# Attention units with transposes in the middle of a slot, three transpose banks and one bank for all value sums

## The chip, the cores and the metric

The kernel runs on one core of a Trainium2 chip. The metric is device time in microseconds (us) of one execution, lower is better. Three runs of the kernel before took 2541.85 us in the median (2540.91 to 2544.57).

The engines in the views are PE (matmul; PEld is its weight load), DVE (vector), ACT (scalar), POOL and SP, which here issues most DMAs. PSUM is the memory that PE writes its results to; it has eight banks, each holding 512 float32 values in each of 128 partitions.

## What is computed

One decoder layer over 2048 tokens of width 1024: an adaLN-modulated RMSNorm, one wide projection, attention in eight heads of width 64 beside a short gated convolution, an output projection, and a convolutional feed-forward part. The change touches the attention alone:

```
fcum = jnp.cumsum(logf, axis=1)
for i in range(s // BLOCK_Q):                       # 16 blocks of 128 queries
    q0, q1 = i * BLOCK_Q, (i + 1) * BLOCK_Q
    logits = jnp.einsum('bqhd,bkhd->bhqk', q[:, q0:q1], k[:, :q1]) * scale
    logits = logits + fcum[:, :, q0:q1, None] - fcum[:, :, None, :q1]
    p = softmax(where(causal, logits, -inf))
    out[i] = jnp.einsum('bhqk,bkhd->bqhd', p, v[:, :q1])
```

Query block i sees i + 1 key blocks of 128. Precision is kept by splitting operands into a high and a low half, so that one product becomes two or three matmuls.

## The kernel before

**Units and slots.** The attention walks over 64 units: head h (eight of them) and u from 0 to 7. A unit pairs query block 15 - u with query block u, so every unit has 17 key blocks of 128. Each unit passes four stages, and the stages of different units share one slot: in slot s (the loop at the end of the attention block) the scores of unit s, the exponentials of unit s - 1, the transposes of unit s - 2 and the value sums of unit s - 4 are written out. Each stage is a Python generator, and the loop takes one step of each in turn ("round 1", "round 2" and so on), in the order in which they stand in the list `run`. The calls marked `K` keep that order on each engine; so the order of the list and the places of the `yield`s set the order of work on PE, DVE and ACT.

**Scores** (L778 to L802). For each chunk of up to 512 keys PE makes two matmuls into a bank of `ps_s` (four banks), and a third one for the causal mask on the last chunk of a query block (L781). DVE adds the forget term and keeps the running maximum (L802). There are five chunks in every unit. PE writes chunks in pairs, one or two ahead of DVE.

**Weights** (L816, L819). ACT scales the maximum (`nb`) and takes two exponentials in place, one for each query block of the pair, with their sums in `l`.

**Turn** (from L825). The weights must be transposed for the value sums. The last eight of the 17 blocks go through POOL (L830, L831 make a high and a low half in `wide`) and a transposing DMA on SP (L832). The first nine blocks go through PE: transposes of 4, 4 and 1 blocks into banks of `ps_x` (L839, inside `blocks`), an ACT copy of the high half out of the bank (L841) and a DVE subtraction for the low half (L846, inside `rest`). Below these are called T0, T4, T8; copy0, copy4, copy8; low0, low4, low8. `ps_x` has two banks, so a new transpose waits for the low half of the one two back.

**Values** (L878 to L880). Three matmuls for each of the 17 blocks add up the value sums of the pair: one bank of `ps_o` (two banks) for each query block. DVE multiplies each with 1/l and writes it to `at` (L869, the function `over`), which is called the eviction below.

**Store** (L895 to L898). After every second head the finished `at` is transposed in four chunks of 512, one in each of four slots: four transposes in a `ps_x` bank, an ACT copy to `tm` (one buffer) and a DMA to `m_at`. `ps_s`, `ps_x` and `ps_o` take eight banks together.

**Other queues.** SP carries, in order, the transposing DMAs, the loads of the next head, the stores and weight loads for the following stage; POOL carries L830 and L831, two copies for each head (L594) and products for the following stage (L675).

Of the kernel before, what the change touches and what calls it, by code (L numbers as in the profile page):

```python
# [8 lines left out]
F32 = mybir.dt.float32  # L9
F32R = mybir.dt.float32r  # L10
F16 = mybir.dt.float16
# [3 lines left out]
ALU = mybir.AluOpType  # L15
AX = mybir.AxisListType
PSUM = bass.MemoryType.PSUM
DRAM = bass.MemoryType.DRAM

P = 128  # L20
# [3 lines left out]
DH = 64  # L24
# [3 lines left out]
NT = S // P  # L28
# [5 lines left out]
WU = (NT + 1) * P  # L34
WB = 9
# [9 lines left out]
def kernel(  # L45
# [20 lines left out]
    V, A, G, T = nc.vector, nc.scalar, nc.gpsimd, nc.tensor  # L66
# [69 lines left out]
    K = tc.keep_in_program_order  # L136
# [10 lines left out]
    with ExitStack() as ph:  # L147
# [32 lines left out]
        with ExitStack() as pa:  # L180
# [110 lines left out]
            for k in range(KD + 2):  # L291
# [4 lines left out]
                if k < KD:  # L296
                    rest = transpose_in(0, k)
# [20 lines left out]
            for ch in range(4):  # L318
# [7 lines left out]
                for t in range(4):  # L326
                    i = ch * 4 + t
# [413 lines left out]
    with ExitStack() as ph:  # L741
        cs = ph.enter_context(tc.tile_pool(name="cs", bufs=6))
        cp = ph.enter_context(tc.tile_pool(name="cp", bufs=2))
        ps_s = st.enter_context(tc.tile_pool(name="ps_s", bufs=4, space=PSUM, side="right"))
        ps_x = ph.enter_context(tc.tile_pool(name="ps_x", bufs=2, space=PSUM))
        ps_o = ph.enter_context(tc.tile_pool(name="ps_o", bufs=2, space=PSUM))

        def load_values(pr):

            v16 = cp.tile([P, NT, 2, P], F16, tag="v16", name="v16")  # L750
            nc.sync.dma_start(v16, v16_sc[pr].rearrange("(t p) a d -> p t a d", p=P))
            return v16

        v16 = [load_values(0)]

        chunks = []
        heads = {0: head}
# [54 lines left out]
        def weights(un):  # L812

            s_t = un["s"]
            nb = cs.tile([P, 2], F32, tag="nb", name="nb")
            K(A.activation(nb, un["mx"], AF.Copy, scale=qk[:, 5:6], bias=LN_PS))  # L816
            for p, (_, n, b0) in enumerate(un["parts"]):
                cols = s_t[:, b0 * P : (b0 + n) * P]
                K(A.activation(cols, cols, AF.Exp, bias=nb[:, p : p + 1], scale=qk[:, 4:5], accum_out=un["l"][:, p : p + 1]))  # L819
                yield  # L820
            un["wide"] = wide = cp.tile([P, 2, WU - WB * P], F16, tag="wide", name="wide", bufs=3)

        def turn(un):

            s_t = un["s"]  # L825
            near = cp.tile([P, 2, WB, P], F16, tag="near", name="near", bufs=3)
            far = cp.tile([P, 2, NT + 1 - WB, P], F16, tag="far", name="far", bufs=3)
            un["t"] = near, far
            wide = un["wide"]
            K(G.tensor_scalar(wide[:, 0, :], s_t[:, WB * P : WU], 1.0, 0.0, op0=ALU.mult, op1=ALU.add))  # L830
            K(G.tensor_tensor(wide[:, 1, :], s_t[:, WB * P : WU], wide[:, 0, :], op=ALU.subtract))  # L831
            nc.sync.dma_start_transpose(far.rearrange("p a b n -> p (a b) n"), wide.rearrange("p a n -> p (a n)"))  # L832
            late = []

            def blocks(b0):
                nb = min(4, WB - b0)
                pt = ps_x.tile([P, 512], F32, tag="x", name="pt")
                for b in range(nb):
                    K(T.transpose(pt[:, b * P : (b + 1) * P], s_t[:, (b0 + b) * P : (b0 + b + 1) * P], ident))  # L839
                th, tl = [near[:, a, b0 : b0 + nb, :].rearrange("p b n -> p (b n)") for a in range(2)]  # L840
                K(A.activation(th, pt[:, 0 : nb * P], AF.Copy))  # L841
                late.append((tl, pt[:, 0 : nb * P], th))

            def rest():
                tl, pt, th = late.pop(0)
                K(V.tensor_tensor(tl, pt, th, op=ALU.subtract))  # L846

            blocks(0)
            blocks(4)
            yield  # L850
            rest()
            yield
            blocks(8)
            rest()
            yield
            rest()
            yield
            K(V.reciprocal(un["l"], un["l"]))

        def values(un):  # L860

            near, far = un["t"]
            h = un["h"]
            sums = []

            def over():
                p, i, po = sums.pop(0)
                o = un["at"][:, i, (h % 2) * DH : (h % 2 + 1) * DH]
                K(V.tensor_scalar(o, po, un["l"][:, p : p + 1], None, op0=ALU.mult))  # L869

            for p, (i, n, b0) in enumerate(un["parts"]):
                po = ps_o.tile([P, DH], F32, tag="o", name="po")
                for b in range(n):
                    g = b0 + b
                    t = near[:, :, g, :] if g < WB else far[:, :, g - WB, :]
                    v = v16[h // 2][:, b, h % 2, :]
                    vh, vl = v[:, 0:DH], v[:, DH:P]
                    K(T.matmul(po, lhsT=t[:, 0, :], rhs=vh, start=b == 0, stop=False))  # L878
                    K(T.matmul(po, lhsT=t[:, 0, :], rhs=vl, start=False, stop=False))
                    K(T.matmul(po, lhsT=t[:, 1, :], rhs=vh, start=False, stop=b == n - 1))  # L880
                    if b % 4 == 3:
                        yield
                        if sums:
                            over()
                sums.append((p, i, po))
            yield
            while sums:
                over()

        def store(at, pr, chs):  # L890

            for ch in chs:
                pt = ps_x.tile([P, 512], F32, tag="x", name="pt")
                for t in range(4):
                    K(T.transpose(pt[:, t * P : (t + 1) * P], at[:, ch * 4 + t, :], ident))  # L895
                tm = cp.tile([P, 512], F32, tag="tm", name="tm", bufs=1)
                K(A.activation(tm, pt, AF.Copy, scale=vi))
                nc.sync.dma_start(m_at[pr][:, ch * 512 : (ch + 1) * 512], tm)  # L898
                yield
# [4 lines left out]
        for s in range(H * nu + 8):  # L904
            h, u = divmod(s, nu)
            run = []
            if h < H:
                if u == 0:
# [3 lines left out]
                    if h % 2 == 0:  # L912
                        if h:
                            v16.append(load_values(h // 2))
                        at = cp.tile([P, NT, P], F32, tag="at", name="at")
                elif h + 1 < H:
                    steps[u - 1]()
                units.append({"h": h, "u": u, "at": at})
            for back, stage in ((2, turn), (0, scores), (1, weights), (4, values)):
                if 0 <= s - back < H * nu:  # L920
                    run.append(stage(units[s - back]))
            if s >= 16 and s % 16 in (0, 4):
                slow.append(store(units[s - 5]["at"], (s - 16) // 16, (0, 3) if s % 16 == 0 else (1, 2)))
# [331 lines left out]
```

## Time and profile before

| | us |
|---|---|
| median of three runs | 2541.85 |
| the profiled execution, its own time | 2541.82 |
| its span in the trace | 2540.1 |
| attention: from the first `nb` (628.55) to the last (973.85) | 345.30 |
| PE busy, DVE busy, ACT busy in that stretch | 307.18, 300.26, 267.44 |

A page of the profile gives busy times over the whole span; answers of the trace give the same for a window, list single instructions, and tell what ended each idle time. "L846 <- ACT near L841" means that the instruction of line 846 waited, and that the last thing it waited for was ACT's write of `near` in line 841. A matmul's row is longer than the distance to the next one, since matmuls overlap; the distance between starts is what one costs. Slots are told apart by the start of `nb` (L816), of which there is one for each unit.

### The profile page before, as it was taken

How to read it: one execution, taken by the hardware profiler on the slowest of the kernel's cores; microseconds unless marked ns; L12 is line 12 of the kernel's file. 1: busy time of each engine (PE TensorE's matmuls, PEld its weight loads, DVE VectorE, ACT ScalarE, POOL GpSimd, SP SyncE). 2: the span in 40 equal slices, each digit the busy share in tenths (PEclk: the TensorE clock that was granted, in tenths of full speed). 3: DMA queues.
4: the chain of work that ended last, by engine and by line, in shares of the span. 5: the costliest groups of instructions: out<-in, count | busy, mean ns of one | idle time of the engine just before them, and what ended most of it. 6: DMA issues, size and time to landing. Idle time of an engine off the chain costs nothing.

```text
span 2540.1 us, 38347 instructions
## 1 busy us (share of the span) xinstructions
PE 2429.5 (96%) x14429; PEld 1988.7 (78%) x14429; DVE 1827.2 (72%) x3422; ACT 1147.2 (45%) x1804; POOL 375.7 (15%) x314
## 2 busy tenths in 40 slices
PE   4999999999989888998999999999999999999999
PEld 4988788887666666877788888887778888888887
DVE  7567874432988886676888888667768888885554
ACT  3522331111778775654444444455534444444333
POOL 4110111111767773110000000000000000000000
PEclk9999999999999999999999999999999999999999
DMA  8332563313799886243222222676742222226775
GB/s 239 141 103 60 149 184 102 97 59 110 145 177 184 167 176 160 81 147 121 75 80 87 83 81 86 204 226 217 218 138 83 83 83 83 83 84 199 225 235 186
DMA packets 416674, 345.62 MB, mean 136 GB/s; under 512 B 182928, under 2 KB 326632, under 8 KB 415464
## 3 DMA queue, kind: packets, MB, share of 16 engines
q1 hardware_dynamic: 409304, 326.33, 45.9%
q10 hardware_dynamic: 4752, 8.46, 0.9%
q0 software_dynamic: 2432, 8.39, 0.9%
q8 instruction: 113, 1.85, 0.3%
q14 instruction: 73, 0.60, 0.1%
HBM read 244.47 MB, written 65.08 MB: 122 GB/s over the span
## 4 chain that ended last, share of the span: by engine, by line
PE 49%; DVE 2%; DMA 1%; ACT 1%; issue 0%; SPq 0%; DVEq 0%; ACTq 0%
PE acc L1103 33%; PE acc L140 15%; DMA t<-x_sc 1%; DVE lo L663 1%; PE pt L991 0%; DVE t L984 0%; DVE t L974 0%; ACT hi L662 0%; DVE t L973 0%; ACT junk L1014 0%; DVE lo L1058 0%; DVE raw L1052 0%; DMA out_dram<-t 0%; DVE b22l L663 0%; SPq L1199 0%
## 5 line engine op out<-in xcount | busy, mean ns | idle before, releaser
L140 PE MATMUL acc<-hi 128*128 128x512 f32 x960 | 378.7, 395 | 10.3 <-ACT hi L662 8.0
L140 PE MATMUL acc<-hi,lo 128*128 128x512 f32 x960 | 376.0, 392 | 1.7 <-DVE lo L663 1.6
L140 PE MATMUL acc<-lo,hi 128*128 128x512 f32 x960 | 375.4, 391 | 0.3 <-DVE lo L663 0.3
L663 DVE TENSOR_TENSOR lo<-raw,hi 128x1024 fp32r<-128x1024 f32 (+1 forms) x208 | 236.0, 1140 | 181.1 <-ACT hi L662 180.6
L662 ACT ACTIVATE hi<-raw 128x1024 fp32r<-128x1024 f32 (+1 forms) x208 | 205.1, 991 | 248.4 <-PE acc L140 206.1
L1116 DVE SCALAR_TENSOR_TENSOR w<-w,fcw,w 128x1024 f32<-128x1024 f32 x176 | 225.8, 1283 | 35.5 <-ACT w L1111 32.2
L1055 ACT ACTIVATE hi<-raw 128x1024 fp32r<-128x1024 f32 x132 | 139.7, 1060 | 211.5 <-PE acc L1103 202.9
L140 PEld LDWEIGHTS acc<-hi 128*128 128x128 f32 x960 | 181.0, 189 | 50.4 <-ACT hi L662 9.2
L140 PEld LDWEIGHTS acc<-hi,lo 128*128 128x128 f32 x960 | 180.8, 188 | 41.7 <-DVE lo L663 3.7
L140 PEld LDWEIGHTS acc<-lo,hi 128*128 128x128 f32 x960 | 181.0, 188 | 37.3 <-DVE lo L663 1.2
L1058 DVE TENSOR_TENSOR lo<-raw,hi 128x1024 fp32r<-128x1024 f32 x132 | 160.9, 1220 | 11.0 <-ACT hi L1055 10.9
L819 ACT ACTIVATE s_t<-s_t,nb,cst 128x2048 f32<-128x2048 f32 (+15 forms) x128 | 164.7, 1287 | 5.7
L140 PE MATMUL pr<-hh,wh 128*128 128x512 f32 x384 | 153.3, 399 | 0.0
L140 PE MATMUL pr<-hl,wh 128*128 128x512 f32 x384 | 151.0, 393 | 0.0
L140 PE MATMUL pr<-hh,wl 128*128 128x512 f32 x384 | 150.7, 392 | 0.0
L846 DVE TENSOR_TENSOR near<-pt,near 128x512 f16<-128x512 f32 (+1 forms) x192 | 106.1, 554 | 44.5 <-ACT near L841 43.2
L831 POOL TENSOR_TENSOR wide<-s_t,wide 128x1024 f16<-128x1024 f32 x64 | 136.6, 2134 | 5.3
L839 PE MATMUL pt<-ident,s_t 128*128 128x128 f32 x576 | 96.9, 288 | 35.0 <-DVE near L846 23.4
L802 DVE CUSTOM_DVE_ANT_0 s_t<-ps,nf,mx 128x512 f32<-128x512 f32 (+1 forms) x192 | 122.7, 639 | 1.2
L778 PE MATMUL ps<-kh,qs 128*128 128x512 f16 (+1 forms) x320 | 111.8, 354 | 2.2 <-ACT bt L635 1.1
L841 ACT ACTIVATE near<-pt 128x512 f16<-128x512 f32 (+1 forms) x192 | 87.2, 480 | 59.0 <-PE pt L839 57.9
L779 PE MATMUL ps<-kl,qs 128*128 128x512 f16 (+1 forms) x320 | 111.9, 354 | 0.0
(303 smaller groups left out, 6200.9 us busy)
## 6 DMA issues: line engine op xcount, KB each, us to landing
raw<-in_w_up_dram SPq DMA_DIRECT2D x88, 512.0 KB, 3.6
raw<-y_sc SPq DMA_DIRECT2D x176, 256.0 KB, 4.0
raw<-in_w_down_dram SPq DMA_DIRECT2D x176, 256.0 KB, 4.3
y_sc<-w SPq DMA_DIRECT2D x44, 512.0 KB, 2.6
wm<-in_w_ada_dram SPq DMA_DIRECT2D x128, 128.0 KB, 2.5
wr<-in_w_in_dram SPq DMA_DIRECT2D x40, 256.0 KB, 4.0
x_t<-in_x_dram SPq DMA_DIRECT2D x16, 512.0 KB, 5.1
wa<-in_w_ada_dram SPq DMA_DIRECT2D x16, 512.0 KB, 6.4
```

Of the source, the lines that this page charges most:

```text
L140: ins = T.matmul(acc, lhsT=a, rhs=b, start=st, stop=sp)
L662: A.activation(hi, raw, AF.Copy, scale=HS)
L663: V.tensor_tensor(lo, raw, hi.bitcast(F32), op=ALU.subtract)
L778: K(T.matmul(ps[:, 0:cw], lhsT=qt, rhs=kh[:, c0 : c0 + cw], start=True, stop=False))
L779: K(T.matmul(ps[:, 0:cw], lhsT=qt, rhs=kl[:, c0 : c0 + cw], start=False, stop=not last))
L802: K(V.tensor_tensor_reduce(out=s_t[:, o0 + c0 : o0 + c0 + cw], in0=ps[:, 0:cw], in1=nf[:, c0 : c0 + cw], scale=1.0, scalar=-3.0e38 if g == ...
L819: K(A.activation(cols, cols, AF.Exp, bias=nb[:, p : p + 1], scale=qk[:, 4:5], accum_out=un["l"][:, p : p + 1]))
L831: K(G.tensor_tensor(wide[:, 1, :], s_t[:, WB * P : WU], wide[:, 0, :], op=ALU.subtract))
L1055: K(A.activation(hi, raw, AF.Copy, scale=HS))
L1058: K(V.tensor_tensor(lo, raw, hi.bitcast(F32), op=ALU.subtract))
L1103: K(T.matmul(acc, lhsT=a, rhs=b, start=st, stop=sp, skip_group_check=True))
L1116: K(V.scalar_tensor_tensor(y, u[:, m : m + 1024], fcw[:, m * 44 + ct : m * 44 + ct + 1], y, op0=ALU.mult, op1=ALU.add))
```

## The change

The pools: `ps_x` gets three banks and `ps_o` one. That one bank is allocated once and cut into four pieces of 2 x 64 columns, used by the units in turn; both query blocks of a unit lie in one piece, and one DVE instruction (L885 after the change) multiplies both with their 1/l. `wide` goes from three buffers to two and `tm` from one to two. In the list, the exponentials come first and the transposes after the scores; the transposes' steps are moved to later rounds.

```diff
@@ -742,8 +742,8 @@
-        ps_x = ph.enter_context(tc.tile_pool(name="ps_x", bufs=2, space=PSUM))
-        ps_o = ph.enter_context(tc.tile_pool(name="ps_o", bufs=2, space=PSUM))
+        ps_x = ph.enter_context(tc.tile_pool(name="ps_x", bufs=3, space=PSUM))
+        ps_o = ph.enter_context(tc.tile_pool(name="ps_o", bufs=1, space=PSUM))
@@ -752,6 +752,8 @@
+        ring = ps_o.tile([P, 512], F32, name="po").rearrange("p (a b d) -> p a b d", b=2, d=DH)
+        rings = [ring[:, a] for a in range(4)]
@@ -818,7 +820,7 @@
-            un["wide"] = wide = cp.tile([P, 2, WU - WB * P], F16, tag="wide", name="wide", bufs=3)
+            un["wide"] = wide = cp.tile([P, 2, WU - WB * P], F16, tag="wide", name="wide", bufs=2)
@@ -845,31 +847,28 @@
+            yield
+            K(V.reciprocal(un["l"], un["l"]))
+            yield
             blocks(0)
+            yield
             blocks(4)
-            yield
-            rest()
             yield
             blocks(8)
             rest()
             yield
             rest()
             yield
-            K(V.reciprocal(un["l"], un["l"]))
+            rest()
 
         def values(un):
-            sums = []
-
-            def over():
-                p, i, po = sums.pop(0)
-                o = un["at"][:, i, (h % 2) * DH : (h % 2 + 1) * DH]
-                K(V.tensor_scalar(o, po, un["l"][:, p : p + 1], None, op0=ALU.mult))
-
+            rings.append(rings.pop(0))
+            po2 = rings[0]
             for p, (i, n, b0) in enumerate(un["parts"]):
-                po = ps_o.tile([P, DH], F32, tag="o", name="po")
+                po = po2[:, p, :]
                 for b in range(n):
@@ -880,12 +879,10 @@
                     if b % 4 == 3:
                         yield
-                        if sums:
-                            over()
-                sums.append((p, i, po))
-            yield
-            while sums:
-                over()
+            yield
+            u = un["u"]
+            o = un["at"][:, NT - 1 - u : u - 1 if u else None : 2 * u + 1 - NT, (h % 2) * DH : (h % 2 + 1) * DH]
+            K(V.tensor_tensor(o, po2, un["l"].unsqueeze(2).broadcast_to([P, 2, DH]), op=ALU.mult))
@@ -893,7 +890,7 @@
-                tm = cp.tile([P, 512], F32, tag="tm", name="tm", bufs=1)
+                tm = cp.tile([P, 512], F32, tag="tm", name="tm", bufs=2)
@@ -916,7 +913,7 @@
-            for back, stage in ((2, turn), (0, scores), (1, weights), (4, values)):
+            for back, stage in ((1, weights), (0, scores), (2, turn), (4, values)):
```

Three places show what moves. The first is ACT in the middle of the attention, before the change: `near<-pt` is copy0, copy4 (128x512) or copy8 (128x128), and `s_t,l<-` are the exponentials.

```order
L819 ACTIVATE s_t,l<-s_t,nb,cst 128x1280
L819 ACTIVATE s_t,l<-s_t,nb,cst 128x896
L841 ACTIVATE near<-pt 128x128
L841 ACTIVATE near<-pt 128x512 x2
L816 ACTIVATE nb<-mx,cst 128x2
L819 ACTIVATE s_t,l<-s_t,nb,cst 128x1152
L819 ACTIVATE s_t,l<-s_t,nb,cst 128x1024
```

The same place on ACT after the change:

```order
L821 ACTIVATE s_t,l<-s_t,nb,cst 128x1280
L821 ACTIVATE s_t,l<-s_t,nb,cst 128x896
L843 ACTIVATE near<-pt 128x512 x2
L843 ACTIVATE near<-pt 128x128
L818 ACTIVATE nb<-mx,cst 128x2
L821 ACTIVATE s_t,l<-s_t,nb,cst 128x1152
L821 ACTIVATE s_t,l<-s_t,nb,cst 128x1024
```

Before, the copy8 of one unit stands right ahead of copy0 and copy4 of the next one; now the three copies of one unit stand together behind the exponentials.

The second place is DVE in one slot, before the change: `s_t,mx<-ps` are the scores' chunks, `near<-pt,near` low0, low4 and low8, and `at<-po,l` the evictions.

```order
L802 ISA s_t,mx<-ps,nf 128x512
L802 ISA mx 128x1
L846 TENSOR_TENSOR near<-pt,near 128x512
L802 ISA s_t,mx<-ps,nf 128x512
L802 ISA mx 128x1
L846 TENSOR_TENSOR near<-pt,near 128x512
L802 ISA s_t,mx<-ps,nf,mx 128x512
L802 ISA mx 128x1
L846 TENSOR_TENSOR near<-pt,near 128x128
L802 ISA s_t,mx<-ps,nf,mx 128x512
L802 ISA mx 128x1
L858 RECIPROCAL l<-l 128x2
```

DVE after the change, from the fourth chunk of one slot to the first of the next:

```order
L804 ISA s_t,mx<-ps,nf,mx 128x512
L804 ISA mx 128x1
L804 ISA s_t,mx<-ps,nf,mx 128x128
L804 ISA mx 128x1
L848 TENSOR_TENSOR near<-pt,near 128x512 x2
L885 TENSOR_TENSOR at<-po,l 128x2x64
L848 TENSOR_TENSOR near<-pt,near 128x128
L804 ISA s_t,mx<-ps,nf 128x512
```

The low halves were spread between the chunks of scores; now they stand behind the last chunk, with the one eviction among them. In half of the units the eviction stands behind low4, as here, in the other half between low0 and low4.

The third place is PE at the start of a slot, before the change: the end of a unit's sums (`far`), two chunks of scores, eight transposes (T0 and T4 together), and the next unit's first sum (`near`).

```order
L880 MATMUL po<-v_7526,far 128x64
L778 LDWEIGHTS qs
L778 MATMUL ps<-kh,qs 128x512
L779 LDWEIGHTS qs
L779 MATMUL ps<-kl,qs 128x512
L778 LDWEIGHTS qs
L778 MATMUL ps<-kh,qs 128x512
L779 LDWEIGHTS qs
L779 MATMUL ps<-kl,qs 128x512
L839 MATMUL pt<-ident,s_t 128x128 x8
L878 LDWEIGHTS near
L878 MATMUL po<-v_7526,near 128x64
```

PE after the change, at the end of a slot: T8, the last block of a unit's sums and the first block of the next unit's.

```order
L841 MATMUL pt<-ident,s_t 128x128
L877 LDWEIGHTS far
L877 MATMUL po<-v_7491,far 128x64
L878 LDWEIGHTS far
L878 MATMUL po<-v_7491,far 128x64
L879 LDWEIGHTS far
L879 MATMUL po<-v_7491,far 128x64
L877 LDWEIGHTS near
L877 MATMUL po<-v_7491,near 128x64
```

The transposes have left the start of the slot for its third, fourth and fifth round. In two units of eight, those with u = 0 and u = 4, nothing stands between the last sum of one unit and the first of the next, and in the built program that first sum of each unit now waits for the eviction of the unit just before it, whose sums lie in the same bank.

## The prediction

> **What bounds the kernel now.** The page first, for the size of the question.
>
> ```profile
> span 2540.1 us, 38347 instructions
> PE 2429.5 (96%) x14429; PEld 1988.7 (78%) x14429; DVE 1827.2 (72%) x3422; ACT 1147.2 (45%) x1804; POOL 375.7 (15%) x314
> PE 49%; DVE 2%; DMA 1%; ACT 1%; issue 0%; SPq 0%; DVEq 0%; ACTq 0%
> ```
>
> PE is busy for 96% of the span and leads the chain that ended last. But this is a mean over stages, and the change touches one of them, so I cut that stage out: windows from the first to the last `nb` of the attention, over one head without stores (eight units), and over single slots.
>
> ```profile
> core 0: us, PE busy (x) PEld busy (x) DVE busy (x) ACT busy (x) POOL busy (x), PEclk, DMA share, GB/s
> 628.55:973.85 345.30, 307.18 (x4423) 231.14 (x4423) 300.26 (x998) 267.44 (x515) 244.89 (x156) 0.98 0.87 171
> 752.14:793.78 41.64, 37.77 (x577) 28.73 (x576) 38.20 (x129) 32.96 (x65) 29.22 (x19) 1.00 0.83 153
> 822.10:830.75 8.65, 5.53 (x63) 4.10 (x62) 5.19 (x17) 4.78 (x10) 8.31 (x6) 0.85 1.13 232
> 830.75:838.04 7.29, 7.29 (x87) 5.46 (x86) 4.92 (x16) 4.09 (x10) 4.18 (x4) 0.71 0.58 112
> ```
>
> The second row is the quiet head: 41.64 / 8 = 5.205 us for a unit, in which PE is busy for 4.72, DVE for 4.78, ACT for 4.12 and POOL for 3.65. No engine is full, so a chain between engines sets the pace. The first row has 63 units: at 5.205 they would take 327.9, so 17.4 us are lost in a few slots, such as the two of the last rows. Who waits for whom in the quiet head:
>
> ```profile
> ACT near L841 <- PE pt L839: 8.4, 9, 1.4
> PE pt L839 <- DVE near L846: 3.6, 7, 0.7
> DVE near L846 <- ACT near L841: 3.2, 5, 0.8
> PE po L878 <- DVE at L869: 0.3, 1, 0.3
> ```
>
> This is a ring. ACT's copies wait for PE's transposes, these for a bank that DVE's low half has to free, and the low half waits for ACT's copy. ACT's rows show the round:
>
> ```profile
> 813.47 0.69 ACT L819 ACTIVATE s_t<-s_t,nb,cst 128x384 f32<-128x384 f32 x1
> 814.16 0.25 ACT L841 ACTIVATE near<-pt 128x128 f16<-128x128 f32 x1
> 814.75 1.34 ACT L841 ACTIVATE near<-pt 128x512 f16<-128x512 f32 x2 [0.33 <-PE pt L839]
> 815.98 0.29 ACT L816 ACTIVATE nb<-mx,cst 128x2 f32<-128x2 f32 x1
> ```
>
> copy8 comes behind the exponentials; low8 follows it; with two banks T4 of the next unit needs the bank that low8 frees; copy4 needs T4; and the next exponentials stand behind copy4. So ACT's 4.12 us of work plus about 1.05 of waiting for transposes (8.4 / 8) give nearly all of the 5.205.
>
> **The change part by part.**
>
> *Three banks and the new order.* With three banks T0, T4 and T8 wait for low0, low4 and low8 of the unit before, a whole slot old, and the exponentials no longer stand between copy8 and the copies that follow from it. The ring is gone. What is late next? ACT needs 4.12, so the candidates are PE and DVE. PE, from the distances between starts:
>
> ```profile
> 809.10 0.38 PE L778 MATMUL ps<-kh,qs 128*128 128x512 f16 x1
> 809.31 0.38 PE L779 MATMUL ps<-kl,qs 128*128 128x512 f16 x1
> 809.53 0.22 PE L781 MATMUL ps<-maskb,ident_b 128*128 128x128 bf16 x1
> 809.59 1.04 PE L839 MATMUL pt<-ident,s_t 128*128 128x128 f32 x8
> 810.66 0.19 PE L878 MATMUL po<-v,near 128*128 128x64 f16 x1
> 810.97 0.19 PE L880 MATMUL po<-v,near 128*128 128x64 f16 x1
> 811.00 0.38 PE L778 MATMUL ps<-kh,qs 128*128 128x512 f16 x1
> ```
>
> A score matmul of 512 columns costs 0.215, a mask 0.06, eight transposes 1.07 (0.134 each), and the twelve sums from 810.66 to 811.00 cost 0.34 (0.0285 each). A unit has 17 x 128 = 2176 columns twice, so 2 x 4.25 x 0.215 = 1.83, two masks 0.12, nine transposes 1.21 and 51 sums 1.46: **4.62 us of PE**. Nothing in the change alters this work.
>
> *One eviction for two.* DVE has now, by its rows in time, and by the view of one line:
>
> ```profile
> 809.45 0.29 DVE L846 TENSOR_TENSOR near<-pt,near 128x128 f16<-128x128 f32 x1 [1.43 <-ACT near L841]
> 809.66 0.74 DVE L802 CUSTOM_DVE_ANT_0 s_t<-ps,nf,mx 128x512 f32<-128x512 f32 x1
> ...
> 810.32 0.28 DVE L869 TENSOR_SCALAR at<-po,l 128x64 f32<-128x64 f32 x1
> 810.52 0.15 DVE L858 RECIPROCAL l<-l 128x2 f32<-128x2 f32 x1
> ...
> 811.79 0.68 DVE L846 TENSOR_TENSOR near<-pt,near 128x512 f16<-128x512 f32 x1
> 812.39 0.68 DVE L802 CUSTOM_DVE_ANT_0 s_t<-ps,nf 128x512 f32<-128x512 f32 x1
> ```
>
> ```profile
> L517 DVE TENSOR_TENSOR qn<-acc,r x32: 683/692/694, 168.7 to 359.4; 128x512 f32<-128x512 f32 x32
> ```
>
> An eviction holds DVE for 0.20 (810.32 to 810.52), two of them 0.40. The new form, a product of a PSUM tile with a broadcast column, is not in the trace at 128 columns. At 512 it takes 692 ns (L517, which is such a product), the same as low0's 0.68 at 512 columns; low8 has 128 columns and holds DVE for 0.21 (809.45 to 809.66). The bounds are 0.20, one old eviction, and 0.69, L517 whole; I take 0.21 since size and kind match low8. DVE falls from 4.78 to 4.59 a unit, below PE's 4.62 plus waits. So the saved 0.19 is hidden by PE, and would cost up to 0.3 more if it came out at 0.69 (only then would DVE be the bound). The reciprocal only moves.
>
> *One bank for all sums: an added wait.* The first sum of each unit now waits for the eviction of the unit before, and PE runs in order, so score chunks and transposes queue behind that sum, and DVE's chunks behind them. What a bare handover costs:
>
> ```profile
> 973.53 0.47 DVE L869 TENSOR_SCALAR at<-po,l 128x64 f32<-128x64 f32 x2
> 973.86 0.19 PE L878 MATMUL po<-v,near 128*128 128x64 f16 x1 [0.54 <-DVE at L869]
> ```
>
> The first of these two evictions ends at 973.53 + 0.28 = 973.81, and PE starts 0.05 later. With 0.05 on the way to DVE too, and 0.16 for the last sum to drain (0.19 less its step), the handover is 0.16 + 0.05 + 0.28 + 0.05 = 0.54. How much of it shows depends on what PE has in between. Laid out by rounds: for u = 1, 2, 5, 6 the sums end in round 4 and PE still has T8 and two score chunks (0.13 + 0.78 = 0.9), so nothing shows. For u = 0 and 4 the sums end in round 5 and the next unit's begin at once: 0.54. For u = 3 and 7 there are 0.9 of work, but the eviction stands behind low4, and low4 behind copy4: after T4 come 0.6 (copy4), 0.6 (low4) and 0.34 with its handover, 1.5 in all, against 0.44 for the last sums plus 0.9, so some 0.2. The mean is (2 x 0.54 + 2 x 0.2) / 8 = 0.19. The bounds are nothing and 0.54 in each unit.
>
> The steps leave something out: for DVE before, they add up to 4.68 (chunks 4.25 x 0.66 = 2.80, low halves 2 x 0.60 + 0.21 = 1.41, reciprocal 0.07, evictions 0.40) where the window has 4.78. I add 0.1 for such small gaps. **A unit then takes 4.62 + 0.19 + 0.10 = 4.91**, and 63 units save 63 x (5.205 - 4.91) = 18.6.
>
> *Two `tm` buffers.* The 17.4 us lost in few slots, in the view of waits, the rows of ACT and PE and a window:
>
> ```profile
> ACT tm L897 <- DMA m_at<-tm: 11.3, 5, 3.1
> 828.37 0.69 ACT L897 ACTIVATE tm<-pt,vi 128x512 f32<-128x512 f32 x1 [3.05 <-DMA m_at<-tm]
> 829.11 0.69 PE L839 MATMUL pt<-ident,s_t 128*128 128x128 f32 x2 [2.76 <-ACT tm L897]
> 828.00:835.00 7.00, 5.89 (x48) 4.21 (x49) 3.67 (x11) 4.78 (x9) 3.87 (x3) 0.52 1.05 206
> ```
>
> The second of two chunks waits until the DMA of the first has read `tm`; ACT stops, PE stops for 2.76, and for 7 us after that PE's granted clock is 0.52, which is why the slot at 830.75 takes 7.29 instead of about 5. With two buffers the second chunk goes on at once. What stays is the work: 12 store chunks lie in the stretch, each with four transposes, 4 x 0.134 = 0.54, so 6.4 us on PE. Saved: 17.4 - 6.4 = 11.0. The `tm` copy (0.6 a step) adds to ACT, which has room.
>
> *Two `wide` buffers.* POOL must now wait until the transposing DMA of two units ago has read `wide`.
>
> ```profile
> L830 POOL TENSOR_SCALAR wide<-s_t x64: 1044/1045/1049, 631.7 to 977.3; 128x1024 f16<-128x1024 f32 x64
> L831 POOL TENSOR_TENSOR wide<-s_t,wide x64: 2118/2134/2144, 632.8 to 978.4; 128x1024 f16<-128x1024 f32 x64
> L832 SPq DMA_TRANSPOSE far<-wide x64: 1767/2884/6888, 635.0 to 980.6; - x64
> DMA to landing us min/median/max: 4.2/4.6/5.7
> ```
>
> It lands 5.7 us after issue at most, and POOL comes back two slots (9.8 us) after it began, with its own 3.2 us (1.04 + 2.13) before the issue; some 1 us of slack, behind it more than a slot until the sums need `far`. Cost nothing, covered by the two slots between transposes and sums; if a load ahead in SP's queue (up to the 6.9 above) uses that up, DVE's chunk of three units later waits for POOL, a few us in total.
>
> **Sum.** The profiled execution took 2541.82 us (span 2540.1), next to the median of 2541.85. 2541.8 - 18.6 - 11.0 = **2512**.
>
> **Rivals.**
>
> *A. Every unit pays the handover.* One bank instead of two leaves no sums that PE could start during an eviction: 4.62 + 0.54 + 0.10 = 5.26 a unit, so 63 x 0.055 = 3.5 lost against now, 11.0 won: 2534. For it: the built program has this wait in each unit. Against: in six of eight units PE has other work there. The Trainium skill says on its page "Perfetto Trace Analysis", section "Matmuls", that independent groups should rotate through different PSUM banks so that one's evacuation overlaps the next one's matmuls; by that rule this rival is the outcome. The trace bears it out so far that PE hardly waits for evictions with two banks (0.3 us in the head above).
>
> *B. Slower: the eviction behind a late low half.* Where low4 waits for copy4, and ACT is behind because the exponentials now stand ahead of all copies, PE's last sums and the eviction stop overlapping: a unit is PE's work, then low4, then the handover: 4.62 + 0.60 + 0.54 + 0.10 = 5.86, and 63 x 0.65 = 41 lost less 11 won gives 2572. It decides as soon as copy4 ends later than PE's last sum in all units, not in two of eight. Against: ACT has 4.12 of work in 4.91, and its exponentials start right after copy8.
>
> *C. The units stay at 5.2*, held by the transposing DMA with two `wide` buffers (DMA share 0.83 in the quiet head, 0.87 over all) or by another ring; only the store stalls go: 2541.8 - 11.0 = 2531.
>
> *D. No handover shows and the small gaps shrink*: 4.70 a unit, 63 x 0.505 = 31.8 and 11.0: 2499. DVE's 4.59 allows it.
>
> **Chances.** Forecast 0.52, A 0.12, B 0.08, C 0.15, D 0.13. The range reaches over A and C above and to D below: 2500 to 2534, which leaves out B, half of A and of D. A measurement can tell about 0.2% (5 us) from no change: the forecast, C, D and half of A are faster (0.86), half of A is about the same (0.06), B is slower (0.08).
>
> **What would show it.** In a head without stores the slots should come down from 5.2 to about 4.9; waits of L841 for `pt` and of `pt` for the low half should be nearly gone, and a wait of the first sum for the eviction should stand in their place, 10 to 15 us in all. The wait of `tm` for its DMA and the clock of 0.5 in mid-attention should be gone. The new eviction should take about 0.29. It is wrong if the first sum waits for more than 0.3 in the mean (A, B), if POOL waits for the transposing DMA (C), or if ACT becomes full.

## The result, and the profile after

The changed kernel takes **2521.26 us** in the median of four runs (2520.23 to 2522.43), the kernel before 2541.76 in four runs beside it (2540.91 to 2544.57). The ratio is 0.9918, with a 95% interval of 0.99 to 0.9935. So the change saves some 20.5 us; the prediction had 29.6. The profiled execution of after took 2520.61 us (2541.82 before).

The page after, again first for the size of the question:

```profile
span 2518.9 us, 38300 instructions
PE 2417.9 (96%) x14429; PEld 1987.5 (79%) x14429; DVE 1818.5 (72%) x3358; ACT 1149.1 (46%) x1804; POOL 375.2 (15%) x314
PE 50%; DVE 2%; DMA 1%; ACT 1%; issue 0%; SPq 0%; ACTq 0%; DVEq 0%
```

It shows almost nothing: PE has 96% of the span as before, and 64 DVE instructions are gone. The windows show the change. They are, in this order: the attention from the first `nb` to the last, one head without stores (eight units), then four single slots.

```profile
core 0: us, PE busy (x) PEld busy (x) DVE busy (x) ACT busy (x) POOL busy (x), PEclk, DMA share, GB/s
630.75:956.10 325.35, 294.04 (x4415) 227.37 (x4415) 290.75 (x936) 268.36 (x514) 244.84 (x156) 0.99 0.93 181
661.55:700.87 39.32, 36.71 (x577) 28.68 (x576) 37.14 (x121) 33.20 (x65) 28.00 (x18) 1.00 0.90 159
681.74:687.23 5.49, 4.84 (x74) 3.59 (x72) 5.49 (x18) 4.32 (x9) 3.36 (x3) 1.00 0.63 89
721.79:727.72 5.93, 5.28 (x78) 4.02 (x76) 5.55 (x18) 4.90 (x10) 3.19 (x2) 1.00 0.93 188
803.27:814.81 11.54, 7.12 (x78) 5.44 (x76) 5.41 (x17) 5.00 (x10) 6.56 (x5) 0.85 1.01 235
892.43:901.80 9.37, 6.71 (x78) 4.69 (x76) 5.53 (x18) 4.90 (x10) 5.18 (x5) 0.85 0.94 182
```

The stretch went from 345.30 to 325.35: 19.95 of the 21.2 us between the two profiled executions lie here. A unit of the quiet head takes 39.32 / 8 = **4.915 us** (5.205 before, 4.91 forecast). So 63 units account for 63 x 0.29 = 18.3. At 4.915 they take 309.6, which leaves 15.7 us lost in few slots, against 17.4 before and 6.4 forecast. The slots say where. All four last rows are of the same place in their head (a unit's length depends on u); the first has no store, the other three have one store chunk each. A store chunk costs 5.93 - 5.49 = 0.44, close to the four transposes that were charged for it. But the two long slots lose 6.05 and 3.88, and these two are most of what stayed. The quiet head is also the quietest of three: the two later heads without stores took 40.00 and 42.21 here, where before all three took 41.6.

```profile
741.83:781.83 40.00, 37.07 (x577) 28.73 (x576) 37.21 (x121) 33.42 (x65) 29.66 (x19) 1.00 0.87 160
828.92:871.13 42.21, 37.50 (x577) 28.81 (x576) 37.56 (x122) 33.41 (x65) 32.82 (x23) 1.00 0.90 177
```

And the first head gains, because the later stages are not there yet at its start: its first eight slots take 36.26, 3.1 less than the quiet head (1.8 less before). So the 15.7 and the 17.4 are sums of losses and this gain.

Who waits in the quiet head of after (engine, what waits and for whom, us in total, times, longest):

```profile
POOL wide L832 <- DMA far<-wide: 6.0, 4, 2.4
ACT near L843 <- PE pt L841: 5.2, 10, 1.1
PE po L877 <- DVE at L885: 2.6, 5, 0.7
DVE near L848 <- ACT near L843: 0.5, 2, 0.2
```

The ring is open: in this head transposes no longer wait for a low half at all (3.6 before), and low halves wait 0.5 for copies (3.2 before). In its place PE's first sum waits 2.6 for the eviction, 0.33 a unit. The same view over the whole attention of after:

```profile
ACT near L843 <- PE pt L841: 40.7, 70, 1.8
POOL wide L832 <- DMA far<-wide: 31.3, 16, 4.9
PE po L877 <- DVE at L885: 19.5, 37, 1.7
DVE near L848 <- ACT near L843: 11.9, 16, 5.5
ACT tm L894 <- PE pt L892: 9.1, 9, 5.1
PE po L877 <- DMA far<-wide: 7.6, 4, 4.0
DVE s_t L804 <- POOL wide L833: 3.6, 4, 1.9
```

No wait of `tm` for its DMA is left (11.3 before). DVE's chunks wait for POOL now and then, 3.6 us in all, which was not so before. And a wait of the value sums for `far`, the data of the transposing DMA, has come, and in the first long slot it looks like this, on PE and on SP's queue:

```profile
810.40 0.23 PE L877 MATMUL po<-v,far 128*128 128x64 f16 x1 [4.04 <-DMA far<-wide]
```

```profile
793.56 4.76 SPq L834 DMA_TRANSPOSE far<-wide  x1
798.36 0.58 SPq L585 DMA_DIRECT2D kl<-k_lo  x1
798.98 0.59 SPq L674 DMA_DIRECT2D wo<-in_w_out_dram  x1
799.67 0.37 SPq L585 DMA_DIRECT2D nf<-nf_sc  x1
800.14 0.38 SPq L895 DMA_DIRECT2D m_at<-tm  x1
800.62 9.90 SPq L834 DMA_TRANSPOSE far<-wide  x2
```

PE stands for 4.04 us until `far` is there. Behind three loads and a store, the two transposing DMAs hold SP for 9.90 us together, against a median of 2.9 for one before. The next rows are the idle stretch of PE and what follows it, a low clock again, as after the store stall of before:

```profile
806.50:810.40 3.90, 0.00 (x0) 0.00 (x1) 1.52 (x5) 0.41 (x1) 0.00 (x0) 0.98 1.08 181
810.40:816.00 5.60, 5.22 (x53) 4.22 (x54) 1.97 (x6) 2.56 (x5) 5.30 (x4) 0.71 0.87 229
```

In the idle stretch the DMA share is 1.08 in the mean (the view's share may come out a little over 1), and behind it PE's granted clock is 0.71 in the mean.

Two smaller answers of the trace: the new eviction, and how long the transposing DMA takes from issue to landing (4.2/4.6/5.7 before).

```profile
L885 DVE TENSOR_TENSOR at<-po,l x64: 277/282/292, 647.8 to 976.2; 128x128 f32<-128x128 f32 x64
```

```profile
DMA to landing us min/median/max: 4.5/5.6/6.7
```

### The profile page after: what moved, and what is told of

It reads as the page before. It is cut to its first block, busy times and chain, and to the rows that moved or that the text cites. A ratio compares the mean times of both kernels' runs of the same rounds, so it can differ in the third digit from the quotient of the medians.

```text
span 2518.9 us, 38300 instructions
## 1 busy us (share of the span) xinstructions
PE 2417.9 (96%) x14429; PEld 1987.5 (79%) x14429; DVE 1818.5 (72%) x3358; ACT 1149.1 (46%) x1804; POOL 375.2 (15%) x314
## 4 chain that ended last, share of the span: by engine, by line
PE 50%; DVE 2%; DMA 1%; ACT 1%; issue 0%; SPq 0%; ACTq 0%; DVEq 0%
PE acc L1100 33%; PE acc L140 16%; DVE lo L663 1%; DMA t<-x_sc 1%; PE pt L988 0%; DVE t L981 0%; DVE t L971 0%; DMA out_dram<-t 0%; ACT junk L1011 0%; DVE t L970 0%; ACT hi L662 0%; DVE b22l L663 0%; DVE lo L1055 0%; DVE t L998 0%; ACT t L990 0%
## 5 line engine op out<-in xcount | busy, mean ns | idle before, releaser
L140 PE MATMUL acc<-wh,hh 128*128 128x512 f32 x256 | 103.6, 405 | 0.0
```

The costliest lines, as they stand in the source:

```text
L140: ins = T.matmul(acc, lhsT=a, rhs=b, start=st, stop=sp)
```

## The experiments

The theory was this: of the 11.0 us of the store stalls only 1.7 came because the DMA engines are nearly full in this stretch. Work on them is about 0.87 x 345.3 = 300 us before and 0.93 x 325.35 = 303 after; the forecast's stretch of about 316 us would have asked for a share of 0.95 in the mean. `tm`'s stall was one place where that jam showed, and with `tm` doubled it shows at `far`. The rivals: that two `wide` buffers instead of three hold POOL back and make `far` late; that SP's queue does it, where a transposing DMA stands behind loads; that the stores cause it. The twelve runs were made in three sets, each on a chip of its own with its own runs of the kernel before. Unless stated, each experiment edits the changed kernel.

### First set: buffers

A third `wide` buffer needs room, so a tile that no instruction uses (`edge`) was cut from 120 to 8 columns in e1_wide3_tm2, and that cut was also run alone.

```diff
# e1_wide3_tm2
-    edge.tile([P, 120], F32, name="edge")
+    edge.tile([P, 8], F32, name="edge")
-            ... tag="wide", name="wide", bufs=2)
+            ... tag="wide", name="wide", bufs=3)
# e2_edge: the first of the two edits only
# e3_wide3_tm1: edge as it was, wide with bufs=3 and tm with bufs=1
# e4_tm1: edge as it was, tm with bufs=1
```

> The changed kernel with three wide buffers instead of two (room for them comes from an unused padding tile, edge, cut from 120 to 8 columns). Theory W: the changed kernel's long slots (803.27, 11.54 us, and 892.43, 9.37 us) come from POOL, which waits 31.3 us for the transposing DMA to free one of two wide buffers, so that the next transposing DMA starts late and PE waits for far. Then PE's wait for far goes from 7.6 us to under 2, POOL's wait for the DMA to under 5, and the time to 2512 +- 3. Rival D: the transposing DMAs are late by themselves, because the loads share their queue and engines and the units come faster; then PE's wait for far stays at 5 us or more and the time within 3 us of 2521.

> The changed kernel with the padding tile alone cut from 120 to 8 columns, two wide buffers as in the change: the control for the run with three. Both theories: 2521 +- 2, no step of the attention moves; a theory that addresses on the right side of SBUF matter would see more than 3 us either way.

> The changed kernel with the buffers of before: three wide, one tm, padding untouched. Theory W: the far stalls go (about -9 us), the tm stalls come back (up to +11, the 11.3 us of ACT's wait for the store's DMA before): 2518 to 2524. Rival D: the far stalls stay and the tm stalls come on top: 2526 to 2533. If the new order alone removes the tm wait (its copy comes later in the slot), W gives 2512 and D 2521.

> The changed kernel with one tm buffer and two wide. If the prediction's term for tm is right, ACT's wait of the tm copy for the store's DMA comes back with 8 to 14 us, PE's clock drops behind it, and the time is 2528 to 2534. Rival: in the new order the store's DMA is through before the next copy, and the time stays within 3 us of 2521.

| kernel | `wide`, `tm` | `edge` | median us (range, runs) | ratio to before, 95% |
|---|---|---|---|---|
| before of this set | 3, 1 | 120 | 2541.5 (2536.33 to 2544.23, 12) | |
| e1_wide3_tm2 | 3, 2 | 8 | 2525.06 (2517.63 to 2526.11, 4) | 0.9935 [0.9918, 0.9953] |
| e2_edge | 2, 2 | 8 | 2529.66 (2525.04 to 2537.54, 8) | 0.9959 [0.9946, 0.9973] |
| e3_wide3_tm1 | 3, 1 | 120 | 2524.12 (2518.94 to 2525.32, 4) | 0.994 [0.9923, 0.9956] |
| e4_tm1 | 2, 1 | 120 | 2530.77 (2524.92 to 2538.47, 5) | 0.9969 [0.9951, 0.9987] |

Against the changed kernel itself (2521.26 above, 2518.25 in the next set), one `tm` buffer instead of two costs some 10 us: e4_tm1 has 2530.77, and its ratio's interval lies above both of the changed kernel's. Its expectation for the case that the forecast's term holds, 2528 to 2534, came true (the wait for the store's DMA, 18.3 us, is above the 8 to 14 expected). The comparisons inside this set say something else, -1.1 us for the second `tm` buffer with two `wide` and +0.9 with three, but there `edge` is cut along with it. And e2_edge, with the cut alone, missed its 2521 by 8.7 us. The traces tell the two apart. Their attention stretch, from the first `nb` to the last:

| `wide`, `tm` | kernel | first and last `nb` | stretch | lost beyond 63 x 4.915 |
|---|---|---|---|---|
| 3, 1 | e3_wide3_tm1 | 628.12, 955.18 | 327.06 | 17.4 |
| 2, 1 | e4_tm1 | 630.42, 963.16 | 332.74 | 23.1 |
| 3, 2 | e1_wide3_tm2 (`edge` cut) | 630.26, 953.82 | 323.56 | 13.9 |
| 2, 2 | the changed kernel | 630.75, 956.10 | 325.35 | 15.7 |
| 2, 2 | e2_edge (`edge` cut) | 631.54, 954.95 | 323.41 | 13.8 |

So what e2_edge takes longer lies outside the attention. Inside it, the second `tm` buffer saved 7 to 9 us with two `wide` buffers and 3.5 with three; giving up the third `wide` buffer cost 5.7 with one `tm` and 2 or nothing with two. Both edits together, from the first row to the fourth, gave 1.7. These are single traces; the changed kernel's second trace, in the next set, has 325.3 too, and its twin with `edge` cut is 1.9 below it, so differences of 2 us mean little.

The first row also holds the order and the banks of the change with the buffers of before. Its stretch is 18.2 us shorter than the 345.30 of before, so these two parts give what the forecast's ring term gives (63 x 0.29 = 18.3), and the 17.4 us in few slots are all still there.

The waits show where the stall stands. In the changed kernel with three `wide` and one `tm` (e3_wide3_tm1):

```profile
ACT tm L894 <- DMA m_at<-tm: 17.3, 5, 4.5
PE pt L841 <- ACT tm L894: 15.1, 7, 3.7
```

and with three `wide` and two `tm` (e1_wide3_tm2), with a window of its longest slot:

```profile
PE po L877 <- DMA far<-wide: 7.5, 2, 4.5
POOL wide L832 <- DMA far<-wide: 10.5, 2, 6.0
```

```profile
886.60:899.60 13.00, 7.86 (x78) 5.76 (x76) 5.58 (x18) 5.06 (x11) 6.80 (x5) 0.76 1.17 151
```

With one `tm` nothing waits for `far` on PE; with two, nothing waits for `tm`'s DMA. The stall stands at the one place or the other, and moving it saved far less than the 11.0 forecast. The third `wide` buffer takes two thirds of POOL's waits away (31.3 to 10.5) and leaves PE's wait for `far` as it was (7.6 and 7.5), so the two buffers are not its cause. What the two buffers do cost stands in the heads without stores: with a third `wide` buffer all three take 39.3, DVE never waits for POOL, and with one `tm` they take 39.3 as well (e4_tm1). Whether the third buffer is worth the 4.6 us (with two `tm`) and 6.6 us (with one) between the medians stays open, since the intervals overlap. Why e2_edge is slower outside the attention, the chip or the shifted addresses, was not separated.

### Second set: what the DMA engines carry, and in which order

```diff
# e5_again: the changed kernel, not edited
# e6_nf_once
+        kept_nf = []
-            t = sp.tile([P, S], F32, tag="nf", name="nf")
-            load(t, nf_sc[h].partition_broadcast(P))
+            if h == 0:
+                kept_nf.append(sp.tile([P, S], F32, tag="nf", name="nf"))
+                load(kept_nf[0], nf_sc[h].partition_broadcast(P))
+            else:
+                steps.append(lambda: None)
+            t = kept_nf[0]
# e7_act_queue: the loads of load_head, and the stores to m_at
-            load = lambda *a: steps.append(lambda: nc.sync.dma_start(*a))
+            load = lambda *a: steps.append(lambda: nc.scalar.dma_start(*a))
-                nc.sync.dma_start(m_at[pr][:, ch * 512 : (ch + 1) * 512], tm)
+                nc.scalar.dma_start(m_at[pr][:, ch * 512 : (ch + 1) * 512], tm)
# e8_store_moved: stores in later slots of the pair
-            if s >= 16 and s % 16 in (0, 4):
-                slow.append(store(units[s - 5]["at"], (s - 16) // 16, (0, 3) if s % 16 == 0 else (1, 2)))
+            if 16 <= s < 64 and s % 16 in (6, 14) or s in (64, 68):
+                slow.append(store(units[s - 5 if s >= 64 else s - 20]["at"], (s - 16) // 16, (0, 3) if s % 16 in (0, 6) else (1, 2)))
```

> The changed kernel once more, on the chip of the runs beside it, since the control of the last set came out 8 us above it. Every theory: within 2521 to 2530; it is the figure that the three others are compared with.

> The changed kernel with the forget term nf loaded for the first head only and used for all heads, which leaves out seven loads of 1 MB (the logits of the other heads get the first head's term). Theory V (the DMA engines are full in the slots where loads, stores and transposing DMAs meet): PE's wait for far, 7.6 us, and the long slots go, POOL's wait for the DMA falls by half or more, time 2511 to 2515 (8 us less than the changed kernel beside it). Rival S (SP's queue holds the transposing DMAs back, since each keeps it for 3 to 5 us and stands behind the others): one short entry of 0.4 us less on SP changes nothing, time within 3 us of the changed kernel.

> The changed kernel with the loads of the next head and the stores to m_at issued from ACT instead of SP; the bytes are the same. Theory S: the transposing DMAs leave SP as soon as POOL is done, far is in time, time 8 us less than the changed kernel beside it. Theory V: the same bytes cross the same DMA engines at the same time, PE's wait for far stays, time within 4 us of the changed kernel, or above it if issuing costs ACT time.

> The changed kernel with the stores of the first three head pairs written out in slots 6, 7, 14 and 15 of the next pair instead of 0, 1, 4 and 5, where the loads of a head, the weight loads and the stores meet. Theory V: DMA work is spread, the long slots (11.5 and 9.4 us) shrink to 5 to 6, time 6 to 9 us less than the changed kernel beside it. Theory S: the same, if the queue is emptier there, since a store is also an entry on SP; a theory that the stalls come from wide alone: no change.

| kernel | median us (range, runs) | ratio to before, 95% |
|---|---|---|
| before of this set | 2541.32 (2538.14 to 2549.23, 13) | |
| e5_again | 2518.25 (2516.4 to 2519.84, 4) | 0.9909 [0.9894, 0.9924] |
| e6_nf_once | 2509.29 (2508.54 to 2510.92, 4) | 0.9875 [0.986, 0.9889] |
| e7_act_queue | 2530.19 (2519.94 to 2537.84, 10) | 0.995 [0.9932, 0.9968] |
| e8_store_moved | 2517.81 (2513.63 to 2519.23, 4) | 0.9904 [0.9886, 0.9923] |

e6_nf_once speaks most clearly. The engines do the same work as before; only seven loads of 1 MB are gone (so the results of seven heads are not those of the layer). First the stretch and the two long slots of e5_again, then those of e6_nf_once, then e6's waits for `far` and the landing of its transposing DMAs:

```profile
630.50:955.80 325.30, 295.04 (x4415) 228.07 (x4415) 290.61 (x936) 268.32 (x515) 244.56 (x156) 0.98 0.94 181
803.20:815.39 12.19, 7.98 (x78) 5.80 (x76) 5.34 (x17) 5.00 (x10) 7.26 (x6) 0.73 1.05 232
891.87:901.68 9.81, 7.11 (x78) 5.21 (x76) 5.61 (x18) 5.02 (x11) 5.12 (x5) 0.83 0.93 156
```

```profile
628.60:943.90 315.30, 290.44 (x4415) 225.16 (x4415) 290.61 (x936) 267.98 (x514) 243.74 (x155) 1.00 0.90 166
799.93:805.86 5.93, 5.27 (x78) 4.03 (x76) 5.54 (x18) 4.90 (x11) 5.76 (x5) 1.00 0.88 193
883.06:889.33 6.27, 5.45 (x78) 4.08 (x76) 5.55 (x18) 4.89 (x10) 3.88 (x3) 1.00 0.98 152
```

```profile
PE po L883 <- DMA far<-wide: 1.2, 2, 1.0
```

```profile
DMA to landing us min/median/max: 4.2/4.3/7.2
```

The DMA work of the stretch falls from 0.94 x 325.3 = 306 to 0.90 x 315.3 = 284 us. The long slots shrink to 5.93 and 6.27, a store slot's ordinary length, and with 6.26 + 3.54 = 9.8 they give nearly all of the 10.0 that the stretch lost. The clock stays at 1.00 in the mean. So the loads of `nf` are what makes these two slots long. The stretch is now 315.3, near what the forecast's terms make of it (309.6 + 6.4 = 316), but that is partly chance: the first head's gain of 3.1 us is in it, and the sixth head, without stores, still takes 41.80, which the loads of `nf` do not explain. POOL's wait for the transposing DMA falls from 34.5 to 23.6 and not by half. The median falls by 9.0 us, and e5_again came out 3 us below its expectation.

e7_act_queue speaks against the order in SP's queue. With the loads out of the transposing DMAs' way in that queue, these became later, not earlier:

```profile
DMA to landing us min/median/max: 4.7/7.6/18.8
```

```profile
PE po L877 <- DMA far<-wide: 11.4, 4, 7.8
```

The kernel got some 12 us slower than e5_again in the median; its runs spread over 18 us, and the trace is of a fast one (2522.82). ACT issues the transfers here, so a part of this may be ACT's own time, and the loads may start at other moments. So the order in SP's queue alone is unlikely, and how much of the jam is full DMA engines and how much that queue is not separated further. e8_store_moved left long slots at the same places, of 9.50 and 9.24 us without a store in them, with the same wait for `far` (7.6; 6.6 in e5_again): the stores are not what makes `far` late. That was expected otherwise; the loads still ran at the old places.

### Third set: the parts of the change, and a mend

```diff
# e9_order: the kernel before, with the change's list `run` and steps of `turn` only
# e10_banks: the kernel before, with the change's pools ps_x and ps_o, rings and values() only
# e11_two_evict: the changed kernel, two evictions out of one bank
-            u = un["u"]
-            o = un["at"][...]
-            K(V.tensor_tensor(o, po2, un["l"].unsqueeze(2).broadcast_to([P, 2, DH]), op=ALU.mult))
+            for p, (i, _, _) in enumerate(un["parts"]):
+                o = un["at"][:, i, (h % 2) * DH : (h % 2 + 1) * DH]
+                K(V.tensor_scalar(o, po2[:, p, :], un["l"][:, p : p + 1], None, op0=ALU.mult))
# e12_spread: e8_store_moved, wide bufs=3, tm bufs=1, edge not cut, and the load of nf kept at its place
-            load(t, nf_sc[h].partition_broadcast(P))
+            steps.append(lambda: K(nc.sync.dma_start(t, nf_sc[h].partition_broadcast(P))))
```

> The kernel before with the new order alone (list and rounds of the transposes), its pools as they were: two transpose banks, two banks for the sums, two evictions, three wide and one tm buffer. Theory B (the third bank is needed): T8 waits for low0 of its own unit, which now stands behind the last chunk of scores on DVE, and exponentials wait behind copy8; a quiet unit takes 5.1 or more, time 2532 to 2540. Rival O (the order alone breaks the ring): a quiet unit takes 4.9, time 2520 to 2526, as the changed kernel with the same wide and tm buffers (2524).

> The kernel before with the new banks alone (three for transposes, one for all sums, one eviction for two), order, wide and tm as they were. Rival O: copy0 and copy4 of the next unit still stand between copy8 and the exponentials, so a quiet unit stays at 5.1 to 5.2, time 2534 to 2542. Theory B: T4 no longer waits for low8 of the unit before, the ring is gone in the old order too, a quiet unit takes 4.8 to 4.95, time 2520 to 2528.

> The changed kernel with the eviction of a unit split in two again (one for each query block), both from the one bank. The forecast's step: DVE has 0.2 us a unit to spare and the time stays within 2 us of the changed kernel (2518 to 2521). Rival: the eviction is part of the handover, so a second one of 0.2 us shows in the four of eight units whose handover shows; 32 x 0.2 = 6 us more, 2524 to 2527.

> A version meant to keep the gain: the changed kernel with three wide buffers and one tm, the stores of the first three pairs in slots 6, 7, 14 and 15, and the load of nf held in program order, so that it is issued in the sixth slot of a head and not with the other loads. If the long slots come from loads, stores and transposing DMAs that meet (theory V), PE waits for far under 2 us, ACT's tm copy for its DMA under 4 us, time 2508 to 2514. If the moved nf load only moves the jam, within 3 us of the changed kernel (2518 to 2521).

| kernel | quiet head, us (a unit) | median us (range, runs) | ratio to before, 95% |
|---|---|---|---|
| before of this set | 41.64 (5.205), from the first trace | 2542.2 (2539.0 to 2547.69, 9) | |
| e9_order | 39.90 (4.99) | 2534.5 (2532.59 to 2539.32, 6) | 0.997 [0.9958, 0.9982] |
| e10_banks | 40.20 (5.03) | 2528.42 (2525.14 to 2533.37, 4) | 0.9944 [0.9924, 0.9964] |
| e11_two_evict | 40.40 (5.05) | 2518.47 (2515.21 to 2521.74, 4) | 0.9899 [0.9876, 0.9922] |
| e12_spread | 39.32 (4.915) | 2517.45 (2514.28 to 2519.3, 4) | 0.9898 [0.9881, 0.9915] |

The new order with the old banks still leaves transposes waiting for a low half, and the new banks with the old order leave the low halves waiting for copies. From the quiet heads of e9_order and of e10_banks:

```profile
661.20:701.10 39.90, 36.88 (x577) 28.75 (x576) 38.53 (x129) 32.99 (x66) 29.22 (x19) 1.00 0.94 160
```

```profile
PE pt L839 <- DVE near L846: 2.5, 4, 0.9
```

```profile
662.00:702.20 40.20, 37.64 (x578) 28.50 (x577) 37.10 (x122) 33.01 (x65) 29.31 (x19) 1.00 0.86 163
```

```profile
DVE near L848 <- ACT near L843: 2.8, 6, 0.9
PE po L875 <- DVE at L883: 1.6, 3, 0.8
```

Either half alone takes most of the ring's cost in a head (-1.74 and -1.44 of -2.32), so each breaks it at another place and together they gain little more there. Both missed what was expected of the unit, and only the time of e9_order lies in an expected range, that of theory B. In total the order alone gains 7.7 us and the banks alone 13.8; both with the same `wide` and `tm` (e3_wide3_tm1) gained 17.4 in their own set. With two transpose banks the order alone loses more in the store slots, where a chunk of the store takes one of the two. From the whole attention of e9_order, then of e10_banks:

```profile
PE pt L839 <- ACT tm L899: 19.6, 13, 4.5
```

```profile
PE pt L841 <- ACT tm L892: 5.1, 4, 2.0
```

(Both have one `tm` buffer, so part of these waits is the store's DMA again.)

In e11_two_evict, the quiet head shows the price of the second eviction: 40.40 - 39.32 = 1.08 for eight units, 0.135 for each.

```profile
660.90:701.30 40.40, 36.93 (x578) 28.70 (x577) 38.51 (x129) 33.44 (x66) 29.20 (x19) 1.00 0.83 158
```

```profile
PE po L877 <- DVE at L885: 3.5, 6, 0.8
```

Over 64 units that would be 8.6 us, yet the time is not worse than that of the changed kernel (ratio 0.9899 against 0.9909 and 0.9918, with overlapping intervals). In its trace the first long slot is gone (6.11 us), another of 7.40 stands in the next head, and the second has 9.53; beyond its own quiet units the stretch loses 7.4 us, where the changed kernel lost 15.7. So slower units seem to leave the DMA more time, and what they lose the jam gives back; that these two are cause and effect fits the theory, but only this one trace speaks to it.

e12_spread was meant to beat both kernels. PE no longer waits for `far`, `tm` waits for its DMA for 5.0 us, and the stretch of its trace is 319.7, 5.6 less than the changed kernel's; but that trace is of its fastest run (2514.28), and its median cannot be told from that of e5_again or e8_store_moved. Of the kernels that do all the work, none is measurably faster than the changed one.

## Why the prediction was partly right

**The ring and the unit: the mechanism right, the exact length by luck.** "A unit then takes 4.62 + 0.19 + 0.10 = 4.91" measured 4.915. PE's work was right (36.71 / 8 = 4.59 busy). But the handover shows with 0.33 in the quiet head and 19.5 / 63 = 0.31 over all, where the rounds gave 0.19 (19.5 us against "10 to 15"), and the 0.1 of small gaps is not seen beside it: 4.59 + 0.33 is already 4.92, so two errors cancel. By its own sign ("more than 0.3 in the mean") the forecast would have been wrong here. Rival A, 0.54 in every unit, falls all the same, although the measured handover lies about half way between the two. The rule quoted with it from the Trainium skill ("Perfetto Trace Analysis", section "Matmuls") points at a cost that the trace bears out, 0.31 us a unit here; but the runs show that this bank was worth more with the transposes: e10_banks pays the handover and is faster than before.

**The eviction: size right, place wrong.** 0.282 against "about 0.29". That its saving "is hidden by PE" was wrong in a quiet head: the eviction lies in the handover, and e11_two_evict lost 0.135 a unit. The term came to nothing in the total all the same, for another reason than the one given.

**Rival C: its sign came, and a little of its effect.** POOL does wait for the transposing DMA, 6.0 us in the quiet head and 31.3 in all, but the units there run at 4.915, not at 5.2. With three buffers the head has the same length (39.31 in e3_wide3_tm1). Two later heads without stores lost 0.7 and 2.9 us, which they did not with three buffers. B and D fall with the unit's measured length.

**The buffers: the step that failed.** "With two buffers the second chunk goes on at once. What stays is the work [...] Saved: 17.4 - 6.4 = 11.0" and, for `wide`, "Cost nothing" gave 1.7 together. The chunk goes on at once, as foretold, and the plain store slots cost what was charged or less (0.44 in the row above). In the traces of the first set the `tm` term alone is worth 7 to 9 us with two `wide` buffers and 3.5 with three, and the `wide` term is not nothing: 5.7 us with one `tm`, 2 or less with two. What was missed is why the store's DMA was late before: 1.05 to 1.13 DMA share stood in the very rows quoted there. With `tm` out of the way the stall appeared at the next user of the DMA, and the clock of 0.5, which should have gone, came back behind it. The sentence "if a load ahead in SP's queue uses that up, DVE's chunk of three units later waits for POOL, a few us in total" saw the load and got its victim right (3.6 us), but missed the larger one: PE's sums wait 7.6 us for `far`. e6_nf_once shows that some 10 us of the stretch come back once 7 MB of loads are away; whether the second `tm` buffer would be worth its 11.0 then was not run. That the 17.4 us were all loss in store slots was also not quite so, since the first head's gain of 1.8 us is in them.

The rest, -1.3 us, lies outside the stretch and was not followed. Which of the other loads beside `nf` matters was not tried.

## What to carry to other kernels

Before a removed DMA wait is credited, look at the DMA share of the slots in which it stands. Here it was over 1 there, although the mean of the stretch was 0.87, and the stall found another victim; seven loads less helped where more buffers did not. A buffer taken away to pay for another one needs a run of its own, and a stage is compared by its stretch in the traces when edits outside it move the whole time. A ring of waits can be broken at several places, and one part of a change often has most of its effect; running each half alone shows what the second is worth.

## What was not expected of the hardware

The granted clock fell after short gaps, and not in proportion to them. In before, PE waited 2.76 us from 826.35; windows of 1 us show 1.00 up to 828 and 0.50 from 829 to 835 (the prediction's window of 7 us begins 1.1 us before PE goes on). In after, PE waited 4.04 us from 806.36; the windows show 1.00 up to 810, 0.50 from 811 to 813 and 1.00 from 814. The shorter wait was followed by the longer slow time. The lost clock added to the price of each long slot.

With the loads issued from a second queue (e7_act_queue) the landing of a transposing DMA of 512 KB took 18.8 us at most (6.7 with all of them on SP), and 7.6 in the median instead of 5.6.
